# Tree attention on one core: loads of Q, K and V put in the order of their use, V copied by half batches

## The chip, the cores and the metric

One core of one Trainium2 chip. The metric is the device time of a launch in microseconds (us); times are medians of several runs, and ratios are taken between runs of the same rounds on the same chip. Engines are called as in the profile: PE is TensorE (PEld its weight loads), DVE is VectorE, ACT is ScalarE, POOL is GpSimd, SP issues the stores. The span is the time from the first to the last instruction of a profiled execution. A half-clock stretch is one in which the trace records a granted TensorE clock of 0.5.

## The reference

Attention over a sequence of 512 whose mask lets each position see itself and its ancestors in a binary tree. Q, K and V are float32, 8 batches x 12 heads x 512 x 64.

```python
mask = np.zeros((seq, seq))
for i in range(seq):
    mask[i, i] = 1
    parent = i
    while parent > 0:
        parent = (parent - 1) // 2
        mask[i, parent] = 1
scores = np.einsum('bhqd,bhkd->bhqk', Q, K) / np.sqrt(dim) + (1 - mask) * (-1e9)
weights = np.exp(scores - scores.max(-1, keepdims=True))
weights = weights / (weights.sum(-1, keepdims=True) + 1e-10)
return np.einsum('bhqk,bhkd->bhqd', weights, V).astype(np.float32)
```

## The kernel before

Work goes by pairs of heads, 6 pairs a batch, 48 in all. POOL issues the loads, which cast float32 to bf16 on the way (the page has 38.24 MB read from HBM and 18.88 MB in the queue of the loads). A load waits for the landing of the load eight places before it, so up to eight are on their way at any time: in the trace the 19th issue began at 27.73 us, 0.28 us after the landing of the 11th load at 27.45. For each pair PE transposes Q and K (`qt`, `kt` are copied out by DVE and ACT), computes scores, ACT exponentiates, PE multiplies with V, and DVE normalizes (`rec`, then `of` in two instructions). Because the mask needs only some keys, V is not used as loaded: DVE copies it into `v1` and `vx`, with 10 small instructions for any number of heads (two on 64 partitions, eight on 32).

```python
def load(b):
    qs = stage.tile([P, H, T * D], bf16); ks = ...
    if b == 0:
        plan = [(Q, b, 0, 2), (K, b, 0, 2), (V, b, 0, 6), (Q, b, 2, 6),
                (K, b, 2, 6), (V, b, 6, H), (Q, b, 6, H), (K, b, 6, H)]
    elif b == 1:
        plan = [(Q, b, 0, 6), (K, b, 0, 6), (V, b, 0, H), (Q, b, 6, H),
                (K, b, 6, H), (V, b + 1, 0, H)]
    elif b < B - 1:
        plan = [(Q, b, 0, 6), (K, b, 0, 6), (V, b + 1, 0, H),
                (Q, b, 6, H), (K, b, 6, H)]
    ...
# the order of work (ACT and PE inside these calls)
for i in range(N):
    b, hp = pairs[i]
    if i + 1 < N: scores(i + 1)
    if i + 3 < N: transposes(i + 3)       # needs Q and K of pair i + 3
    values(i)                             # PE, then rec, of, of on DVE, then the store
    if b == 0: ...
    elif b + 1 < B:                       # the copies of the next batch's V
        if hp == 0: todo = spread(b + 1, 0, H)
        cuts = (0, 1, 2, 4, 6, 8, 10)
        copies(todo[cuts[hp]:cuts[hp + 1]])
```

Of the kernel before, what the change touches and what calls it, by code (L numbers as in the profile page):

```python
# [126 lines left out]
def kernel(  # L127
# [8 lines left out]
    B, H, S, D = Q.shape  # L136
# [64 lines left out]
    def load(b):  # L201
        qs = stage.tile([P, H, T * D], bf16)
        ks = stage.tile([P, H, T * D], bf16)
        if b == 0:
            plan = [(Q, b, 0, 2), (K, b, 0, 2), (V, b, 0, 6), (Q, b, 2, 6),
                    (K, b, 2, 6), (V, b, 6, H), (Q, b, 6, H), (K, b, 6, H)]
        elif b == 1:
            plan = [(Q, b, 0, 6), (K, b, 0, 6), (V, b, 0, H), (Q, b, 6, H),
                    (K, b, 6, H), (V, b + 1, 0, H)]
        elif b < B - 1:  # L210
            plan = [(Q, b, 0, 6), (K, b, 0, 6), (V, b + 1, 0, H),
                    (Q, b, 6, H), (K, b, 6, H)]
        else:
            plan = [(Q, b, 0, 6), (K, b, 0, 6), (Q, b, 6, 10), (K, b, 6, 10),
                    (Q, b, 10, H), (K, b, 10, H)]
        for src, n, h0, h1 in plan:
            if src is V:
                if n not in loaded_v:
                    loaded_v[n] = stage.tile([P, H, T * D], bf16, name="vs")
                dst = loaded_v[n]  # L220
            else:
                dst = qs if src is Q else ks
            nc.gpsimd.dma_start(  # L223
                out=dst[:, h0:h1, :],
                in_=src[n, h0:h1].rearrange("h (p t) d -> p h (t d)", t=T),
            )
        loaded[b] = (qs, ks)

    def pick(v, t0, t1):

        stop = t1 + (1 if t1 > t0 else -1)
        return v[:, :, t0:stop if stop >= 0 else None:t1 - t0, :]

    def spread(b, h0, h1):
        vs = loaded_v[b]
        v1, vx = v1s[b % NV], vxs[b % NV]
        v = vs[:, h0:h1, :].rearrange("p h (t d) -> p h t d", t=T)
        ops = [
            (vx[64:P, h0:h1, 0:3:2, 0:D], v[64:P, :, 0:3:2, :]),
            (vx[0:64, h0:h1, 1:4:2, 0:D], v[64:P, :, 1:4:2, :]),  # L240
        ]
        for part, c, t0, t1 in ((0, 0, 1, 2), (32, 0, 3, 0), (64, 1, 2, 1),
                                (96, 1, 0, 3)):
            assert KORD[XW[c] + part // 32] == (t0, 1)
            assert KORD[XW[c + 2] + part // 32] == (t1, 1)
            ops.append((
                vx[part:part + 32, h0:h1, c:c + 3:2, 0:D],
                pick(v[32:64], t0, t1),
            ))
        for r in range(T):  # L250
            ops.append((
                v1[32 * r:32 * r + 32, h0:h1, 0:D],
                v[0:32, :, KORD[K1 + r][0], :],
            ))
        return ops

    def copies(ops):
        for o, i in ops:
            nc.vector.tensor_copy(out=o, in_=i)  # L259

    pairs = [(b, hp) for b in range(B) for hp in range(HP)]
    state = {}

    def transposes(i):
        b, hp = pairs[i]
        if hp == 0:
            load(b)
        qs, ks = loaded[b]
        tq = psumT.tile([P, 512], bf16)
        tk = psumT.tile([P, 576], bf16)  # L270

        def put(o, src, t, mat):
            for hi in range(2):
                nc.tensor.matmul(  # L274
                    out=o[D * hi:D * hi + D], rhs=perms[mat],
                    lhsT=src[:, 2 * hp + hi, D * t:D * t + D],
                    start=True, stop=True, is_transpose=True,
                )

        put(tq[:, 64:192], qs, 0, 1)  # L280
        put(tq[:, 0:384].rearrange("d (c x) -> d c x", c=2)[:, :, 0:64], qs, 1, 0)
        for t in range(2, T):
            put(tq[:, P * t:P * t + P], qs, t, 0)
        for t in range(T):
            at = kput[t][1]
            if at[1] - at[0] == 32:
                step, run = at[2] - at[0], 64
            else:
                step, run = at[1] - at[0], 32
                assert at[2] - at[1] == step  # L290
            o = tk[:, at[0]:]
            o = bass.AP(o.tensor, o.offset, [list(o.ap[0]), [step, P // run], [1, run]])
            put(o, ks, t, 2 + t)
        qt = work.tile([P, 512], bf16)
        kt = work.tile([P, 512], bf16)
        nc.vector.tensor_copy(out=qt[:, :], in_=tq[:, :])  # L296
        nc.scalar.copy(  # L297
            out=kt[:, :].rearrange("d (i j x) -> d i j x", j=2, x=32),
            in_=tk[:, :].rearrange("d (j i x) -> d i j x", j=2, x=32)[:, 0:8],
        )  # L300
        state[i] = (qt, kt)

    def scores(i):
        b, hp = pairs[i]
        q_, k_ = state[i]
        st1 = psumS.tile([P, 2, 512], fp32)
        stx = psumS.tile([P, 2, 512], fp32)

        def mm(dst, lhsT, rhs, first):
            nc.tensor.matmul(  # L310
                out=dst, lhsT=lhsT, rhs=rhs, start=first, stop=True,
                skip_group_check=not first,
            )

        hb = [slice(D * hi, D * hi + D) for hi in range(2)]
        q = [q_[hb[hi], :] for hi in range(2)]
        k = [k_[hb[hi], :] for hi in range(2)]
        for hi in range(2):
            mm(st1[:, hi, :], ck1[hb[hi], :], cq1[hb[hi], :], True)
        for hi in range(2):  # L320
            mm(st1[:, hi, :], k[hi][:, 32 * K1:32 * K1 + P], q[hi], False)
        et1 = et1pool.tile([P, 2, 512], bf16)
        nc.scalar.activation(  # L323
            out=et1[:, :, :], in_=st1[:, :, :], func=AF.Exp, scale=scale
        )
        for hi in range(2):
            mm(stx[:, hi, 0:384], ckx[hb[hi], :], cqx[hb[hi], :], True)
        for c in range(T):
            for hi in range(2):
                mm(stx[:, hi, 96 * c:96 * c + 96],  # L330
                   k[hi][:, 32 * XW[c]:32 * XW[c] + P],
                   q[hi][:, P * c + 32:P * c + P], False)
        etx = etxs[i % NX]
        nc.scalar.activation(  # L334
            out=etx[:, :, :, 32:P],
            in_=stx[:, :, 0:384].rearrange("p h (c q) -> p h c q", c=T),
            func=AF.Exp, scale=scale,
        )
        state[i] = (et1, etx)
# [35 lines left out]
    N = len(pairs)  # L375
    E = mybir.EngineType
    with tc.manual_schedule(engines={E.PE, E.DVE, E.Activation, E.Pool}):
        transposes(0)
        scores(0)
        transposes(1)  # L380
        copies(spread(0, 0, 6))
        transposes(2)
        for i in range(N):
            b, hp = pairs[i]
            if i + 1 < N:
                scores(i + 1)
            if i + 3 < N:
                transposes(i + 3)
            values(i)
            if b == 0:  # L390
                if hp in (0, 3):
                    todo = spread(0, 6, H) if hp == 0 else spread(1, 0, H)
                copies(todo[4 * (hp % 3):4 * (hp % 3) + 4])
            elif b + 1 < B:
                if hp == 0:
                    todo = spread(b + 1, 0, H)
                cuts = (0, 1, 2, 4, 6, 8, 10)
                copies(todo[cuts[hp]:cuts[hp + 1]])


# [28 lines left out]
```

## Time and profile before

| | before |
|---|---|
| time, median of 4 runs | 160.02 us (158.96 to 160.46) |
| profiled span | 159.3 us |
| DVE busy | 121.9 us |
| V copies on DVE | 90 |
| last load landed | 137.0 us |

Most lines that matter are shown in the prediction. One is kept for here: the chain that ended last, by engine. It is followed back from the last instruction, at each step to whatever released it.

```profile
DMA 63%; DVE 19%; PE 8%; POOL 4%; issue 3%; POOLq 0%
```

The chain goes back over some 50 us of work without waits for loads, to the K that landed at 109.64, and from there only from landing to landing. Read alone it says that loads set the time. DVE's timeline says that the engine was rarely short of work even so. Both are true of a kernel in which two resources are nearly in balance.

### The profile page before, as it was taken

What the parts mean: (1) busy time and instruction counts of PE and PEld (TensorE: products, weight loads), DVE (VectorE), ACT (ScalarE), POOL (GpSimd) and SP (SyncE); (2) the same over time, 40 slices, a digit from 0 to 9 for tenths busy, and PEclk for the clock granted to TensorE, in tenths of its full rate; (3) what the DMA queues carried; (4) which work ended last, traced back from release to release, by engine and by line L of the source; (5) the groups of instructions that cost most, each with busy time, mean ns of one, the idle gap of its engine ahead of it and who ended that gap; (6) DMA issues with size and microseconds to landing.
All of it is one profiled execution on the core that took longest, in us unless ns stands there. A gap on an engine that the chain in (4) does not pass through costs nothing.

```text
span 159.3 us, 5182 instructions
## 1 busy us (share of the span) xinstructions
PE 112.5 (71%) x2208; PEld 80.9 (51%) x2208; DVE 121.9 (77%) x291; ACT 107.5 (67%) x145; POOL 39.1 (25%) x49
## 2 busy tenths in 40 slices
PE   0357497743998789865996699644998599759730
PEld 0224365532766566543774467423676476547520
DVE  2109499899689989995799799971699989997651
ACT  3053559565488779882898689851598879887820
POOL 7965450422232233032212332203301000000000
PEclk9999969999599999998799999995599999999995
DMA  5999999999999999999999999999999999323331
GB/s 136 148 182 196 197 199 220 223 238 217 225 224 223 237 226 237 234 237 225 217 227 238 225 240 226 242 221 240 199 220 236 228 238 221 126 83 121 136 128 69
DMA packets 50951, 32.28 MB, mean 203 GB/s; under 512 B 1520, under 2 KB 50800, under 8 KB 50928
## 3 DMA queue, kind: packets, MB, share of 16 engines
q0 software_dynamic: 37584, 18.88, 87.6%
q1 hardware_dynamic: 13344, 13.08, 28.5%
q8 instruction: 17, 0.28, 0.7%
q14 instruction: 6, 0.05, 0.1%
HBM read 38.24 MB, written 12.58 MB: 319 GB/s over the span
## 4 chain that ended last, share of the span: by engine, by line
DMA 63%; DVE 19%; PE 8%; POOL 4%; issue 3%; POOLq 0%
DMA ks<-in_K_dram 44%; DMA qs<-in_Q_dram 19%; DVE of L363 11%; PE o L352 4%; DVE vx L259 3%; POOL qs L223 2%; DVE rec L358 2%; DVE v L259 2%; DVE qt L296 2%; POOL ks L223 1%; PE st L310 1%; POOL vs L223 1%; PE tk L274 1%; PE stx L310 1%; PE tq L274 1%
## 5 line engine op out<-in xcount | busy, mean ns | idle before, releaser
L323 ACT ACTIVATE et<-st 128x1024 bf16<-128x1024 f32 x48 | 49.2, 1025 | 26.5 <-PE st L310 26.0
L363 DVE TENSOR_TENSOR of<-o,rec 128x512 f32<-128x512 f32 x96 | 53.2, 554 | 3.3
L352 PE MATMUL o<-v,et 128*128 128x65 bf16 x384 | 31.8, 199 | 18.6 <-DVE of L363 12.2
L297 ACT COPY kt<-tk 128x512 bf16<-128x512 bf16 x48 | 28.4, 592 | 17.8 <-PE tk L274 17.8
L352 PEld LDWEIGHTS <-et 128*128 128x128 bf16 x384 | 25.9, 100 | 25.9 <-DVE of L363 16.8
L334 ACT ACTIVATE etx<-stx 128x768 bf16<-128x768 f32 x48 | 38.6, 805 | 0.0
L352 PE MATMUL o<-vx,etx 128*128 128x65 bf16 x384 | 31.5, 198 | 0.0
L274 PE MATMUL tq<-ptile,qs 128*64 128x128 bf16 x384 | 21.4, 237 | 13.5 <-DMA qs<-in_Q_dram 9.3
L296 DVE COPY qt<-tq 128x512 bf16<-128x512 bf16 x48 | 20.3, 422 | 13.1 <-PE tq L274 12.1
L259 DVE COPY vx<-vs 32x1536 bf16<-32x1536 bf16 (+3 forms) x54 | 28.5, 527 | 1.2
L274 PE MATMUL tk<-ptile,ks 128*64 128x128 bf16 x384 | 21.2, 235 | 9.8 <-DMA ks<-in_K_dram 9.5
L352 PEld LDWEIGHTS <-etx 128*128 128x128 bf16 x384 | 26.7, 100 | 0.0
L310 PEld LDWEIGHTS <-kt 64*128 64x128 bf16 x480 | 19.4, 100 | 9.5 <-issue 2.6
L223 POOL DMA_DIRECT2D qs<-in_Q_dram x18 | 15.1, 836 | 35.0 <-DMA vs<-in_V_dram 12.9
L274 PEld LDWEIGHTS <-qs 128*64 128x64 bf16 x384 | 14.9, 116 | 17.1 <-DMA qs<-in_Q_dram 10.5
L223 POOL DMA_DIRECT2D ks<-in_K_dram x18 | 15.1, 841 | 31.9 <-DMA ks<-in_K_dram 10.4
L358 DVE RECIPROCAL rec<-o 128x8 f32<-128x8 f32 x48 | 9.6, 200 | 15.0 <-PE o L352 15.0
L274 PEld LDWEIGHTS <-ks 128*64 128x64 bf16 x384 | 15.3, 119 | 11.2 <-DMA ks<-in_K_dram 10.8
L310 PE MATMUL st<-ctile 64*128 64x512 bf16 x96 | 20.2, 417 | 0.0
L310 PE MATMUL st<-qt,kt 64*128 64x512 bf16 x96 | 19.7, 407 | 0.1
L310 PE MATMUL stx<-qt,kt 64*128 64x96 bf16 x384 | 17.2, 212 | 0.0
L310 PE MATMUL stx<-ctile 64*128 64x384 bf16 x96 | 16.9, 348 | 0.0
(11 smaller groups left out, 35.7 us busy)
## 6 DMA issues: line engine op xcount, KB each, us to landing
out_dram<-of SPq DMA_DIRECT2D x48, 256.0 KB, 6.3
qs<-in_Q_dram POOLq DMA_DIRECT2D x14, 384.0 KB, 27.2
ks<-in_K_dram POOLq DMA_DIRECT2D x14, 384.0 KB, 26.2
vs<-in_V_dram POOLq DMA_DIRECT2D x7, 768.0 KB, 28.2
vs<-in_V_dram POOLq DMA_DIRECT2D x2, 384.0 KB, 8.4
qs<-in_Q_dram POOLq DMA_DIRECT2D x2, 256.0 KB, 15.4
ks<-in_K_dram POOLq DMA_DIRECT2D x2, 256.0 KB, 15.2
ctile<-tree_codes SPq DMA_DIRECT2D x1, 288.0 KB, 2.9
```

Source lines behind the costliest of these rows:

```text
L223: nc.gpsimd.dma_start(out=dst[:, h0:h1, :], in_=src[n, h0:h1].rearrange("h (p t) d -> p h (t d)", t=T),)
L259: nc.vector.tensor_copy(out=o, in_=i)
L274: nc.tensor.matmul(out=o[D * hi:D * hi + D], rhs=perms[mat], lhsT=src[:, 2 * hp + hi, D * t:D * t + D], start=True, stop=True, is_transpos ...
L296: nc.vector.tensor_copy(out=qt[:, :], in_=tq[:, :])
L297: nc.scalar.copy(out=kt[:, :].rearrange("d (i j x) -> d i j x", j=2, x=32), in_=tk[:, :].rearrange("d (j i x) -> d i j x", j=2, x=32)[:, 0:8],
L310: nc.tensor.matmul(out=dst, lhsT=lhsT, rhs=rhs, start=first, stop=True, skip_group_check=not first,)
L323: nc.scalar.activation(out=et1[:, :, :], in_=st1[:, :, :], func=AF.Exp, scale=scale)
L334: nc.scalar.activation(out=etx[:, :, :, 32:P], in_=stx[:, :, 0:384].rearrange("p h (c q) -> p h c q", c=T), func=AF.Exp, scale=scale,)
L352: nc.tensor.matmul(out=o2[:, hi, (D + 1) * t:(D + 1) * (t + 1)], lhsT=e, rhs=v, start=n == 0, stop=n == len(w) - 1,)
L358: nc.vector.reciprocal(out=rec[:, :, :, :], in_=o4[:, :, :, D:D + 1])
L363: nc.vector.tensor_tensor(out=of4[p0:p1, :, t0, :], in0=o4[p0:p1, :, c0, 0:D], in1=rec[p0:p1, :, c0, :].to_broadcast([p1 - p0, 2, t0.stop, ...
```

## The change

The intent is that no load stands in the queue ahead of one needed sooner: for each group of three pairs Q, K, then V. Since V now comes only a group ahead of its use, it can no longer be copied for a whole batch at a time. It is copied by half batches, over the three pairs ahead of its use; the copies of one half batch, with the pairs that they are laid over, are called a spread below.

```diff
--- before.py
+++ after.py
@@ -203,16 +203,14 @@
         ks = stage.tile([P, H, T * D], bf16)
         if b == 0:
             plan = [(Q, b, 0, 2), (K, b, 0, 2), (V, b, 0, 6), (Q, b, 2, 6),
-                    (K, b, 2, 6), (V, b, 6, H), (Q, b, 6, H), (K, b, 6, H)]
-        elif b == 1:
-            plan = [(Q, b, 0, 6), (K, b, 0, 6), (V, b, 0, H), (Q, b, 6, H),
-                    (K, b, 6, H), (V, b + 1, 0, H)]
-        elif b < B - 1:
-            plan = [(Q, b, 0, 6), (K, b, 0, 6), (V, b + 1, 0, H),
-                    (Q, b, 6, H), (K, b, 6, H)]
+                    (K, b, 2, 6)]
         else:
-            plan = [(Q, b, 0, 6), (K, b, 0, 6), (Q, b, 6, 10), (K, b, 6, 10),
-                    (Q, b, 10, H), (K, b, 10, H)]
+            plan = [(Q, b, 0, 6), (K, b, 0, 6), (V, b, 0, 6)]
+        if b < B - 1:
+            plan += [(Q, b, 6, H), (K, b, 6, H), (V, b, 6, H)]
+        else:
+            plan += [(V, b, 6, H), (Q, b, 6, 10), (K, b, 6, 10),
+                     (Q, b, 10, H), (K, b, 10, H)]
         for src, n, h0, h1 in plan:
             if src is V:
                 if n not in loaded_v:
@@ -387,15 +385,12 @@
             if i + 3 < N:
                 transposes(i + 3)
             values(i)
-            if b == 0:
-                if hp in (0, 3):
-                    todo = spread(0, 6, H) if hp == 0 else spread(1, 0, H)
-                copies(todo[4 * (hp % 3):4 * (hp % 3) + 4])
-            elif b + 1 < B:
-                if hp == 0:
-                    todo = spread(b + 1, 0, H)
-                cuts = (0, 1, 2, 4, 6, 8, 10)
-                copies(todo[cuts[hp]:cuts[hp + 1]])
+            if i - i % 3 + 3 < N:
+                if i % 3 == 0:
+                    nb, nh = pairs[i + 3]
+                    todo = spread(nb, 2 * nh, 2 * nh + 6)
+                cuts = (0, 3, 6, 10)
+                copies(todo[cuts[i % 3]:cuts[i % 3 + 1]])
 
 
 # ---- launch: one core; inputs and outputs as the reference has them ----
```

> **What bounds the kernel now.** I read the page first (engines, slices), then the waits, then VectorE's timeline, then the groups by form and the trace's landing of every load.
>
> ```profile
> PE 112.5 (71%) x2208; PEld 80.9 (51%) x2208; DVE 121.9 (77%) x291; ACT 107.5 (67%) x145; POOL 39.1 (25%) x49
> PEclk9999969999599999998799999995599999999995
> DMA  5999999999999999999999999999999999323331
> ```
>
> The queues are full until slice 34 (136 us), where the last loads land, yet the kernel runs 23 us longer. So transfers do not set the end directly. DVE is the busiest engine at 77%. The clock row shows short stretches at half speed.
>
> ```profile
> ACT et L323 <- PE st L310: 26.0, 29, 3.2
> DVE rec L358 <- PE o L352: 15.0, 17, 3.4
> PE tk L274 <- DMA ks<-in_K_dram: 9.5, 7, 2.3
> ```
>
> DVE's waits in the middle of the run are few. The longest one, 3.4 us, is this, in DVE's timeline (start, duration):
>
> ```profile
> 105.75 0.72 DVE L259 COPY v<-vs 32x768 bf16<-32x768 bf16 x2
> 107.50 0.42 DVE L296 COPY qt<-tq 128x512 bf16<-128x512 bf16 x1 [1.03 <-PE tq L274]
> 111.35 0.21 DVE L358 RECIPROCAL rec<-o 128x8 f32<-128x8 f32 x1 [3.43 <-PE o L352]
> ```
>
> TensorE waited there for Q and K of batch 5's second half, queued behind the whole V of batch 6; that K landed at 109.64. This is what the change aims at. Away from such places DVE runs without a gap:
>
> ```profile
> 46.29 0.19 DVE L358 RECIPROCAL rec<-o 128x8 f32<-128x8 f32 x1
> 46.51 1.14 DVE L363 TENSOR_TENSOR of<-o,rec 128x512 f32<-128x512 f32 x2
> 47.69 1.11 DVE L259 COPY vx<-vs 32x1536 bf16<-32x1536 bf16 x2
> 48.83 0.42 DVE L296 COPY qt<-tq 128x512 bf16<-128x512 bf16 x1
> 49.17 0.20 DVE L358 RECIPROCAL rec<-o 128x8 f32<-128x8 f32 x1
> ```
>
> One pair takes 1.76 us of fixed DVE work plus its share of V copies, here 2.88 in all. The last pairs, which have no copies, come every 2.14 us, TensorE's own pace. So the kernel is bound by DVE almost throughout, with a few transfer stalls on top. I model it as a chain of output issues, read from the trace: first at 21.1 us; batch 0's six periods 19.4 (they carry one and a half batches of V copies); batches 1 to 6 at 15.6 each (measured undisturbed in batch 6: 2.33, 2.21, 2.89, 2.90, 2.37, 2.88); five periods of 2.14; 3.35 from the last output to the end. Sum 148.0. Losses, as excess of single periods: waits for K 1.6 + 0.4 + 3.4 = 5.4; half-clock stretches 4.3; V copies held up beside load issues about 2. That makes 159.7 against 159.3 measured, so the chain holds.
>
> [...] both queues' packet time is 87.6% and 28.5% of the span, over 100% together; [...]
>
> ```profile
> L259 DVE COPY vx<-vs 32x1536 bf16<-32x1536 bf16 x28 | 15.5, 554 | 0.6
> L259 DVE COPY v<-vs 32x768 bf16<-32x768 bf16 x28 | 10.3, 369 | 0.4
> L259 DVE COPY v<-vs 32x384 bf16<-32x384 bf16 x8 | 2.8, 349 | 0.1
> ```
>
> Half of 554 is 277, but a free 768 copy takes 0.353 us and a free 384 copy 0.25 (the 349 holds collisions). [...] beside the load issue at 27.73 two small copies took 0.83 us,
>
> ```profile
> 27.78 0.83 DVE L259 COPY v<-vs 32x384 bf16<-32x384 bf16 x2
> 25.49 0.51 DVE L259 COPY v<-vs 32x384 bf16<-32x384 bf16 x2
> ```
>
> against 0.51 for two with no issue beside them. [...] a copy that writes partitions 0 up right before the qt copy lets qt start 0.08 early (45.95, while the copy runs to 46.03); where the copy ends in a higher quadrant qt starts 0.03 late.
>
> **The change part by part.**
>
> *Loads.* The bytes stay 37.7 MB read. Groups of three pairs get Q, K, V in order, 384 KB each. From 22.6 to 130.8 us before, 38 such units landed, 2.85 us each, so a group lands every 8.54. Batch 0's second Q and K move ahead of its V by one unit: K lands at 16.66, not 18.62. TensorE does these transposes before the first values, but the tq buffer is free only at 16.97, so the first output comes at 19.7: **1.4 us gained**. Placing the new order on the measured landings by bytes, group 3's K lands at 30.2 and is needed at 34.8; group 6's at 56.3, needed at 61.5; group 12's at 109.6, needed at 114.9. Each V lands 3 us later and is needed 2.7 us later. So there are four to five us in hand everywhere and the **5.4 us of waits for K go**.
>
> *Copies.* Batches 1 to 7 have 10 copies each, all heads at once; batch 0 has 20. Now every batch has 20: 160 instead of 90. A full batch costs 6 x 0.554 + 4 x 0.353 = 4.74 us; two halves cost 2 x (6 x 0.353 + 4 x 0.25) = 6.24, with 0.013 between copies some 6.4. Seven batches: **about +11.4 us of DVE work**, on the engine that sets the pace.
>
> *Wait at the end of each spread.* TensorE's values of the next group read v1, which the last copies finish. Before, at each batch end, the period was 2.88 with only 0.73 of copies: copies, then 0.67 of matmuls, then the reciprocal. That is 2.15 + copies rather than 1.76 + copies. It now comes 15 times rather than 8: about +2.7.
>
> *Periods.* Pair 0 of a group: 1.76 + 3 x 0.366 - 0.10 (qt not held) = 2.76. Pair 1: 2.86. Pair 2: 2.15 + 4 x 0.264 - 0.11 (first v copy not held) = 3.10. A group takes **8.72 us**, 2.91 per pair, against 15.6/6 = 2.60.
>
> *Sum.* 19.7 + 15 groups x 8.72 (130.8) + 2 x 2.14 + 3.35 = 158.1 us undisturbed. Half-clock stretches: a throttled pair took 3.4 to 3.6 before, so each costs 0.6 instead of 1.1 to 1.3; I take 2.0. Copies beside load issues: [...] Over a period of 2.95 the chance times the cost is 0.11 us an issue; some 36 issues follow 19 us, a few in idle time, so 3.4 (my estimate). Span 163.5; the timed median was 0.5 above the profiled span, so **164.0 us**.
>
> **Rivals.**
> *The stalls go and little is paid.* If DVE had slack for the extra copies, 159.8 - 5.4 - 1.4 = 153. For it: DVE is at 77%, and in the chain of waits DMA has 63%. Against: that chain strings landings together, each behind the load eight places before, and the periods show DVE without a gap outside some ten places.
> *V just in time becomes a new wait.* DVE now waits in line for each V at pair 0 of the group ahead. At 8.72 us of work for 8.54 us of transfer it is close to balance; if loads slow to 3.1 us a unit, the last V lands near 145, and with three pairs with and three without copies behind it the time is about 162: not far from mine by another mechanism. Against: the lead of 4 us from the start, which grows.
> *Few collisions.* From 42 to 120 us before, issues cost copies only 0.25 us in 26 issues (one copy or two in a row, luck of phase). Then 160.5 to 161.5: within 2%.
> *Phases lock.* Issues and pairs both recur every 2.9 us; if they lock badly, 0.3 x 36 gives 11 us and 170.
>
> **Range and chances.** The base 158.1 is good to 1.5, the clock to 1, the collisions to 2.5, together about 3: 160.5 to 167.5. Two per cent faster (under 156.6) would need less than the undisturbed chain, chance 0.04. Slower starts at 163.0, just under my value: 0.60; the same 0.36.
>
> **What would show it.** DVE copies of V x160, no 1536 form, busy of DVE near 133 us; the first output near 19.7; DVE's rec waits short, with none of 3.4 us behind a landing; outputs every 8.7 to 9 us a group from 20 to 150; loads landing well before use and the DMA row falling off near 136 again, with compute 25 us behind. Wrong if DVE sits idle for V or K (rival two), if groups take under 8.5 us, or if small copies beside load issues last no longer than free ones.

## The result

| | before | after |
|---|---|---|
| time, median of 4 runs | 160.02 us (158.96 to 160.46) | 164.8 us (164.11 to 165.57) |
| profiled span | 159.3 us | 162.3 us |
| DVE busy | 121.9 us | 131.3 us |
| V copies on DVE | 90 | 160 |
| last load landed | 137.0 us | 137.0 us |
| first output issued | 21.1 us | 20.1 us |

The ratio is 1.031, 95% interval 1.023 to 1.039: 3% slower. (A ratio is the mean time of one kernel's fast runs over that of the other's of the same rounds, so it is not quite the ratio of the medians quoted.)

The engines, the clock and the DMA row of the changed kernel's page:

```profile
PE 112.3 (69%) x2208; PEld 81.4 (50%) x2208; DVE 131.3 (81%) x361; ACT 106.5 (66%) x145; POOL 42.4 (26%) x56
PEclk9999999699999999999999598799999999999695
DMA  5999999999999999999999999999999996123131
```

The queues run dry at the same time as before, at 137 us; the work ends 25 us later instead of 22. The chain that ended last has turned over:

```profile
DVE 65%; PE 19%; issue 7%; DMA 5%; POOL 1%; DVEq 0%; POOLq 0%
```

From the first output on there is no landing left in it. The waits (total, times, longest) show what took the place of the wait for K:

```profile
PE o L350 <- DVE v L257: 25.4, 15, 2.3
...
DVE rec L356 <- PE o L350: 9.2, 21, 1.2
...
PE tk L272 <- DMA ks<-in_K_dram: 1.0, 2, 0.7
```

PE's wait for K is down from 9.5 us to 1.0, and `rec` no longer waits over 1.2 us anywhere. PE now waits 15 times for the v copies, once for each group. DVE's timeline of one group, from the first copies of one to those of the next (start, duration):

```profile
38.61 1.09 DVE L257 COPY vx<-vs 64x768 bf16<-64x768 bf16 x3
39.63 0.40 DVE L294 COPY qt<-tq 128x512 bf16<-128x512 bf16 x1
...
41.35 1.08 DVE L257 COPY vx<-vs 32x768 bf16<-32x768 bf16 x3
42.47 0.42 DVE L294 COPY qt<-tq 128x512 bf16<-128x512 bf16 x1
...
44.11 1.03 DVE L257 COPY v<-vs 32x384 bf16<-32x384 bf16 x4
45.17 0.42 DVE L294 COPY qt<-tq 128x512 bf16<-128x512 bf16 x1
45.89 0.21 DVE L356 RECIPROCAL rec<-o 128x8 f32<-128x8 f32 x1 [0.30 <-PE o L350]
...
47.31 1.09 DVE L257 COPY vx<-vs 64x768 bf16<-64x768 bf16 x3
```

DVE works without a gap but one: after the four v copies and `qt` it waits 0.30 us for the values of the next group, which could not begin before those copies ended. (PE's 25 us of waits for the copies are no measure of the loss: in e3 below they are gone, and PE waits 30.7 us for `of` instead.) In the first period `qt` starts 0.07 us before the three copies in front of it end, in the second 0.04 after; the last copy writes from partition 0 in the one case and from a higher one in the other, the same two cases as in the prediction. In this trace `qt` started 0.07 us early each of the 15 times that it followed such a copy to partition 0; what causes this was not shown. The group takes 8.70 us, and so does each of the next three.

The same copies by form (busy, mean ns of one, idle before):

```profile
L257 DVE COPY vx<-vs 32x768 bf16<-32x768 bf16 x64 | 23.5, 367 | 1.1
L257 DVE COPY v<-vs 32x384 bf16<-32x384 bf16 x64 | 16.9, 265 | 0.7
L257 DVE COPY vx<-vs 64x768 bf16<-64x768 bf16 x32 | 11.4, 357 | 0.7
```

They add up to 51.8 us, where the copies before (all six forms) added up to 41.5. A free copy of 768 elements takes 0.351 us and one of 1536 elements 0.551, so an estimate of the fixed part of a copy is 2 x 0.351 - 0.551 = 0.15 us; 70 more copies at 0.15 are 10.5 us, about the 10.3 of the difference.

### The profile page after: what moved, and what is told of

The parts are those of the page before. It is cut to its first block, busy times and chain, and to the rows that moved or that the text cites. A ratio compares the mean times of both kernels' runs of the same rounds, so it can differ in the third digit from the quotient of the medians.

```text
span 162.3 us, 5259 instructions
## 1 busy us (share of the span) xinstructions
PE 112.3 (69%) x2208; PEld 81.4 (50%) x2208; DVE 131.3 (81%) x361; ACT 106.5 (66%) x145; POOL 42.4 (26%) x56
## 4 chain that ended last, share of the span: by engine, by line
DVE 65%; PE 19%; issue 7%; DMA 5%; POOL 1%; DVEq 0%; POOLq 0%
DVE of L361 29%; DVE vx L257 15%; PE o L350 11%; DVE v L257 10%; DVE qt L294 6%; DMA qs<-in_Q_dram 5%; DVE rec L356 4%; PE st L308 3%; PE tq L272 2%; PE stx L308 2%; PE tk L272 1%; POOL qs L221 1%; POOL vs L221 1%; POOL ks L221 0%; DVEq L361 0%
## 5 line engine op out<-in xcount | busy, mean ns | idle before, releaser
L257 DVE COPY vx<-vs 32x768 bf16<-32x768 bf16 (+1 forms) x96 | 34.9, 364 | 1.8
L294 DVE COPY qt<-tq 128x512 bf16<-128x512 bf16 x48 | 20.1, 418 | 11.3 <-PE tq L272 10.4
L272 PE MATMUL tk<-ptile,ks 128*64 128x128 bf16 x384 | 21.1, 235 | 1.3 <-DMA ks<-in_K_dram 1.0
L221 POOL DMA_DIRECT2D qs<-in_Q_dram x18 | 14.6, 814 | 26.3 <-DMA ks<-in_K_dram 18.8
L221 POOL DMA_DIRECT2D vs<-in_V_dram x16 | 13.4, 835 | 27.2 <-DMA qs<-in_Q_dram 19.1
L257 DVE COPY v<-vs 32x384 bf16<-32x384 bf16 x64 | 16.9, 265 | 0.7
```

The costliest lines, as they stand in the source:

```text
L221: nc.gpsimd.dma_start(out=dst[:, h0:h1, :], in_=src[n, h0:h1].rearrange("h (p t) d -> p h (t d)", t=T),)
L257: nc.vector.tensor_copy(out=o, in_=i)
L272: nc.tensor.matmul(out=o[D * hi:D * hi + D], rhs=perms[mat], lhsT=src[:, 2 * hp + hi, D * t:D * t + D], start=True, stop=True, is_transpos ...
L294: nc.vector.tensor_copy(out=qt[:, :], in_=tq[:, :])
```

## The experiments

Theory: the change loses through its copies (70 more instructions, each with a fixed cost, on the engine that sets the pace, and a spread that ends right before its use), while its order of loads by itself gains. Main rival: V just in time is the loss, through new waits for loads. Seven kernels and one repetition ran. The times of the kernel before in these rounds were 159.1 to 163.8 us, its fast runs 159.1 to 161.6. The kernels were timed in rounds other than those of the changed kernel, so where two ratios are set against each other, the rounds differ.

### e1: one step of the new order alone

Edit of the kernel before:

```diff
         elif b < B - 1:
-            plan = [(Q, b, 0, 6), (K, b, 0, 6), (V, b + 1, 0, H),
-                    (Q, b, 6, H), (K, b, 6, H)]
+            plan = [(Q, b, 0, 6), (K, b, 0, 6), (Q, b, 6, H),
+                    (K, b, 6, H), (V, b + 1, 0, H)]
```

> The kernel before with one thing of the new order: in batches 2 to 6 the second half of Q and K is issued ahead of the next batch's V. Copies stay as before (whole batches, 90 copies, 10 a batch). Theory (the change lost through its copies, not through its order): DVE work stays at 122 us, the 3.4 us wait for K of batch 5 goes, but the whole V now lands last of its batch, and the first copy of it may wait about 2.7 us at the first pair of each batch. Counted from landings (a batch of loads every 17.1 us) the end comes at a span of 150 to 156, timed 152 to 158, so 1 to 5% faster than before. Rival (order of use by itself makes new waits for V and costs as much as it saves): 160 to 165, with DVE waiting for V in most batches.

Measured: 158.84 us, ratio to before 0.994 (0.988 to 1.000), span 156.9. The order does not cost, but a gain is hardly clear of the noise (the verdict by the 2% line is the same time), and it is less than expected: time and span lie just outside the expected ranges. The wait of 3.4 us is gone (no `rec` waits over 2.2 us), and a part of it has come back as a wait for V. DVE's timeline where batch 6 begins:

```profile
123.76 1.14 DVE L363 TENSOR_TENSOR of<-o,rec 128x512 f32<-128x512 f32 x2
126.44 0.56 DVE L259 COPY vx<-vs 64x1536 bf16<-64x1536 bf16 x1 [1.54 <-DMA vs<-in_V_dram]
```

The first copy of the last V waited 1.54 us for that V, which landed at 126.4, and 30 us of work follow it. So the rival has something in it, for an order that loads V whole.

### e2: the new copies alone

The loads of the kernel before, with the changed kernel's loop:

```diff
-            if b == 0: ...
-            elif b + 1 < B: ...
+            if i - i % 3 + 3 < N:
+                if i % 3 == 0:
+                    nb, nh = pairs[i + 3]
+                    todo = spread(nb, 2 * nh, 2 * nh + 6)
+                cuts = (0, 3, 6, 10)
+                copies(todo[cuts[i % 3]:cuts[i % 3 + 1]])
```

> The loads of the kernel before, the copies of the changed kernel (160 half-batch copies spread over the three pairs ahead of use). Theory (the copies carry the loss): the groups take 8.7 us as in the changed kernel, first output near 21, so timed 164 to 167.5, the same as the changed kernel or up to 1.5% slower. At 17.4 us of DVE work a batch against 17.1 us of loads most of the 5.4 us of waits for K disappear even with the old order. Rival (the loss comes from the order of the loads, V just in time): near the kernel before, 159 to 161.

Measured: 167.71 us, ratio 1.049 (1.041 to 1.058). So the copies alone cost 4.9%, about 7.9 us of 160.2. The change as a whole costs 3.1%; by these two ratios the order of the loads gives back 1.8%, about 2.9 us, beside these copies. (The two ratios come from different rounds; their intervals do not overlap.) The time is just above the expected range. I had expected most of the waits for K to be absorbed, and they were not. The waits of e2:

```profile
PE o L352 <- DVE v L259: 22.0, 13, 2.3
...
DVE rec L358 <- PE o L352: 12.1, 20, 2.2
...
PE tk L274 <- DMA ks<-in_K_dram: 6.7, 5, 2.3
```

PE still waited 6.7 us for K, against 1.0 in the changed kernel and 9.5 before.

### e3: the same copies one pair earlier

Edit of the changed kernel (`load` of a batch is called a little sooner in the program so that its V exists; the order of the issues is the same):

```diff
-            if i - i % 3 + 3 < N:
-                if i % 3 == 0:
-                    nb, nh = pairs[i + 3]
+            j = i + 1
+            if j - j % 3 + 3 < N:
+                if i == 0 or j % 3 == 0:
+                    nb, nh = pairs[j - j % 3 + 3]
                     todo = spread(nb, 2 * nh, 2 * nh + 6)
                 cuts = (0, 3, 6, 10)
-                copies(todo[cuts[i % 3]:cuts[i % 3 + 1]])
+                copies(todo[0 if i == 0 else cuts[j % 3]:cuts[j % 3 + 1]])
```

> The changed kernel with each group's copies moved one pair earlier, so that the four v copies end a pair before TensorE's values read them. Same 160 copies, same loads in the same order. Theory (each spread that ends right before its use costs 2.15 - 1.76 = 0.39 us, 15 times): group 8.3 us instead of 8.7, timed 157.5 to 160.5, some 3% faster than the changed kernel; TensorE's waits for the v copies (25 us in all) fall to near nothing. Rival (transfers set the pace, V just in time): needing V 3 us earlier makes DVE wait for it, and the time stays at 164 or rises.

Measured: 159.22 us, ratio 0.998 (0.990 to 1.007), span 157.4: 3.3 points under the changed kernel's ratio, with the same 160 copies and the same loads. DVE's timeline of a group there:

```profile
76.73 1.03 DVE L257 COPY v<-vs 32x384 bf16<-32x384 bf16 x4
77.79 0.42 DVE L294 COPY qt<-tq 128x512 bf16<-128x512 bf16 x1
78.14 0.20 DVE L356 RECIPROCAL rec<-o 128x8 f32<-128x8 f32 x1
```

`rec` follows `qt` with no wait, and outputs come every 8.31 us a group (68.52, 76.83, 85.14, 93.45). Fifteen times 0.39 is 5.9 us; from the first to the 46th output the traces have 127.7 us here and 133.9 in the changed kernel, while the first output came 1.1 us later here. So the wait at the end of each spread is real and of the size predicted, though it costs DVE nothing that its busy time would show. The two executions also differ in their clock (0.98 here, with no half-clock stretch between 21 and 151 us, and 0.944 there), but the 8.31 and the 8.70 are both read where nothing disturbs the groups.

The rival's waits for V do not appear: DVE has none on a V in this trace. From 28 to 43 us five pairs took 15.05 us where undisturbed ones take 13.90, with DVE at work without a gap; the 1.15 us more are five V copies that lasted longer beside load issues. One of them is among these three (at 73.98 three such copies took 1.08 us):

```profile
31.24 1.32 DVE L257 COPY vx<-vs 32x768 bf16<-32x768 bf16 x3
```

In the whole trace 14 copies after 19 us were prolonged, by 2.5 us together.

### e4: without the v copies (wrong result on purpose)

```diff
-        nc.vector.memset(v1s[i][:, :, D:VW], 1.0)
+        nc.vector.memset(v1s[i][:, :, :], 1.0)
...
-                copies(todo[cuts[i % 3]:cuts[i % 3 + 1]])
+                copies(todo[cuts[i % 3]:min(6, cuts[i % 3 + 1])])
```

> Wrong result on purpose: the changed kernel without the 4 v copies of each group (after batch 0's first half), the v tiles filled with ones once. Loads unchanged. Theory (DVE sets the pace of the changed kernel, and right under it lie the loads): DVE work of a group falls to 1.76 + 1.1 + 1.76 + 1.1 - 0.1 plus 2.14 = 7.8 us, less than the 8.54 us of a group's loads, so now loads bind: waits for Q and K at group starts, DMA busy to about 137, end about 12 us behind the last landing: timed 150 to 154. Rival (loads or V just in time bind the changed kernel already): 162 to 165.

Measured: 157.81 us, ratio 0.985 (0.979 to 0.992), span 155.9. The result was wrong, as intended. The ratio is 4.6 points under that of the changed kernel, so DVE did set the pace of the changed kernel. (Against the kernel before, the 2% line leaves the verdict unclear.) But 60 copies of 0.25 us and fifteen waits of 0.39 are 21 us, and only some 7 came back. The waits show where the rest stayed:

```profile
PE tk L272 <- DMA ks<-in_K_dram: 7.1, 9, 1.4
...
DVE vx L257 <- DMA vs<-in_V_dram: 2.5, 6, 0.8
```

With only a little less work on DVE the loads bind. My expected 150 to 154 was too low: the last load landed at 139.1, not 137, and the span ended 17 us behind it, not 12, because two pairs with copies and a half-clock stretch (137.8 to 141.2 us) still lay in the tail. A second thing shows here. In this trace 18 V copies after 19 us lasted longer than their form does otherwise, 4.6 us in all; in the changed kernel it was 5 copies and 1.4 us. One of them is among the copies of the first fence, with the load issue beside it in the second:

```profile
60.87 1.29 DVE L257 COPY vx<-vs 64x768 bf16<-64x768 bf16 x3 [0.56 <-DMA vs<-in_V_dram]
```

```profile
61.13 0.88 POOL L221 DMA_DIRECT2D ks<-in_K_dram  x1 [2.18 <-DMA vs<-in_V_dram]
```

The same landing of V released the copies and the next load issue, so they met. DVE waited for the landing of a V at six places in this trace. This is one way in which the two fall into step, and not the only one: e3 has 14 such copies without any wait for V, while e1 and e5 to e7, with 90 to 100 copies, most of them larger, have 3 to 7.

### e5, e6, e7: towards a version that beats both

e5 takes e1 and treats only the last batch's V as the change does: in halves, the second half behind the last batch's first Q and K.

```diff
-                    (K, b, 6, H), (V, b + 1, 0, H)]
+                    (K, b, 6, H), (V, b + 1, 0, H if b + 2 < B else 6)]
...
-            plan = [(Q, b, 0, 6), (K, b, 0, 6), (Q, b, 6, 10), (K, b, 6, 10),
-                    (Q, b, 10, H), (K, b, 10, H)]
+            plan = [(Q, b, 0, 6), (K, b, 0, 6), (V, b, 6, H), (Q, b, 6, 10),
+                    (K, b, 6, 10), (Q, b, 10, H), (K, b, 10, H)]
...
+            elif b + 2 >= B:
+                if hp == 0:
+                    todo = spread(B - 1, 0, 6) if b + 1 < B else spread(b, 6, H)
+                cuts = (0, 0, 3, 6, 8, 10, 10) if b + 1 < B else (0, 5, 10, 10, 10, 10, 10)
+                copies(todo[cuts[hp]:cuts[hp + 1]])
```

> e1 (Q and K of the second half ahead of the next batch's whole V, whole-batch copies for batches 1 to 6), with the last batch's V alone loaded and copied in halves as in the changed kernel: first half in batch 6, second half behind the last batch's first Q and K, copied over its first two pairs. Theory (in e1 the end hangs on the landing of the whole last V at 126.4 us, with 15.6 us of DVE work for a batch and 14 us of tail behind it; half of it lands 3 us earlier and half the copies move to where DVE has slack): span 153.5 to 156, timed 155.3 to 158, 2 to 3% faster than the kernel before. Rival (order and granularity of V at the end do not matter, e1 is bound by something else): within 0.5% of e1, so 0.99 to 1.0 of before.

Measured: 159.16 us, ratio 0.987 (0.982 to 0.993), span 156.2. It is 1.3% faster than the kernel before, which is clear of the noise but under the 2% line; the timed value is above the expected range, and at 158.5 to 159.4 its runs lie beside those of e1 (158.4 to 159.8); a gain over e1 is not shown.

e6 also moves batch 0's second Q and K ahead of its second V:

```diff
-                    (K, b, 2, 6), (V, b, 6, H), (Q, b, 6, H), (K, b, 6, H)]
+                    (K, b, 2, 6), (Q, b, 6, H), (K, b, 6, H), (V, b, 6, H)]
```

> e5 with batch 0's second Q and K ahead of its second V, as in the changed kernel. Theory: the first output comes 1.4 us earlier, but in the middle of the run loads bind (a batch per 17.1 us against 15.6 of DVE work), so the end moves by less than 1 us against e5: 0 to 0.6% faster than e5. Rival (DVE binds throughout, so a gain at the start is kept to the end): 1.4 us, 0.9% faster than e5.

Measured: 159.70 us (18 runs), ratio 0.995 (0.991 to 0.999). The first output came at 18.8 us instead of e5's 21.3, but at the first output of batch 2 e6 was at 56.95 to e5's 56.83, and at that of batch 6 at 125.3 to 125.2. The gain at the start was used up on the way, and the end was no earlier: the ratio is 0.8 points above e5's, where 0 to 0.6% faster had been expected, though the intervals just overlap. That loads took the gain, as expected, is not shown. From 32 to 44 us, where most of it went, e6 has no wait of PE or DVE for a load; it has a half-clock stretch of 10.2 us (32.4 to 42.6; e5 has 3.4 us there), in which `rec` waited 1.7 us for PE, and one copy prolonged by 0.2 us beside a load issue.

e7 lets the copies of batches 2 to 6 begin two pairs later, so as not to wait for V:

```diff
-                cuts = (0, 1, 2, 4, 6, 8, 10)
+                cuts = (0, 0, 0, 3, 6, 8, 10)
```

> e6 with the copies of batches 2 to 6 begun at the third pair of the batch instead of the first. Theory (in e5 and e6 the whole V, landing last of its batch's loads, is waited for by the first copy: the V of batch 6 at 108.9 us, and 16.2 us of DVE work behind it set the output at 125.2, although Q and K had landed five us before): the output at the start of batch 6 comes at 123 to 124, the end two us earlier, span near 154.5, timed 156 to 158, 2 to 3% faster than the kernel before. Rival (a later start of the copies only packs them into fewer pairs and costs as much as it saves): 159 to 161, the same as e6 or slower.

Measured: 160.15 us (22 runs), ratio 0.996 (0.993 to 0.999): the same as e6, and the rival was right. The output at the start of batch 6 came at 126.1, not 123 to 124. DVE no longer waited for a V (2.9 us in e6), but two pairs without copies leave it idle:

```profile
111.29 0.41 DVE L296 COPY qt<-tq 128x512 bf16<-128x512 bf16 x1
112.12 0.21 DVE L358 RECIPROCAL rec<-o 128x8 f32<-128x8 f32 x1 [0.42 <-PE o L352]
112.36 1.14 DVE L363 TENSOR_TENSOR of<-o,rec 128x512 f32<-128x512 f32 x2
113.53 1.69 DVE L259 COPY vx<-vs 64x1536 bf16<-64x1536 bf16 x3
```

A pair without copies takes PE's 2.14 us, so 0.4 us of DVE time is lost in it, and the four other pairs carry more. Batches 2 to 5 took 16.9 to 17.7 us each, about the 17.1 us of a batch's loads; which of the two set them is not separated. The ratios of e1, e5, e6 and e7 lie within 1% of each other.

### The changed kernel again

> The changed kernel once more, for a second trace. Theory: DVE group period 8.7 us where nothing disturbs it, whatever the clock and the phase do; the time copies lose beside load issues depends on how issue and copy phases drift, 1.4 us in the first trace between 20 and 150 us, and may be anything from 0.5 to 4 here. Rival (collisions are fixed by the program): 1.4 us again at the same pairs.

Measured once, without rounds: 161.99 us, span 160.2. Where nothing disturbs it the group takes 8.70 us again (37.13 to 45.83). Prolonged copies after 19 us cost 1.0 us, at other places than before (three between 22 and 28 us, two at 101 and 104), so collisions are not fixed by the program. This execution had its first output at 18.8 us and fewer half-clock stretches before the end than the first; a single run doesn't settle how often. Its time is below all four timed runs (164.1 to 165.6), beside a kernel before whose fast runs were 159.1 to 161.4 in the rounds of that chip. So the loss may be smaller in some executions than the 3.1%; one run of unknown state cannot say. Of the 2.1 us between the two spans 1.3 lie before the first output.

## Why the prediction was right

It forecast 164.0 us, slower, and 164.8 was measured. The mechanism is the one that it named; that the total came so near is in part luck, since two errors, of 1.3 and 2.0 us, went in opposite directions (the last points). By its steps:

- **First output** at 19.7: 20.1 in the profiled run, 18.8 in the second trace.
- **Periods** 2.76, 2.86 and 3.10 us, group 8.72: measured 2.74, 2.86 and 3.09, group 8.69 (output issues at 38.61, 41.35, 44.21, 47.30). This carried the prediction, and it rested on durations that batch 0 of the kernel before already showed for half-batch copies.
- **Waits for K vanish**: right. V was in hand too: the copies at 47.31 used a V landed at 42.28, those at 110.09 one landed at 101.70. The hand was 5 us and grew to 8.
- **DVE work**, +11.4 us with the gaps between copies: the copies' own time rose by 10.3 (10.5 by its sum without gaps), DVE's busy time to 131.3, not 133.
- **The wait at the end of each spread**, 0.39 us fifteen times: shown by e3.
- **The copies cost more than the order gains**: shown by e2. That the order gains beside these copies follows from e2 and the change itself. In the traces of e2 and of the changed kernel, whose spans differ by 2.4 us, 1.2 lie before the first output and 1.4 between it and the 46th; the latter hold half-clock stretches too, so the share of the waits for K is not separated.
- **Collisions of copies with load issues**, 3.4 us: mis-sized, 1.4 measured (1.0 in the second trace). The 0.11 us an issue behind it was my estimate, with issues and copies taken to meet at random. Between 42 and 71 us issues came every 2.87 us and pairs every 2.90, so that they drifted past each other slowly, and no copy was prolonged; of the five that were, three stood between 91 and 98 us. In e4, e3 and e2 it was 4.6, 2.5 and 1.4 us, so the guess was not off everywhere.
- **Half-clock stretches**, 2.0: the outputs from first to 46th took 133.9 us; fifteen groups of 8.70 are 130.5, collisions 1.4, which leaves 2.0. About 1.4 of it lies in or beside the stretches that the clock records show, and 0.5 at the first pair, where PE was late. From the 46th output to the end it took 8.3 us, not 7.6, with 4.9 of them at half clock.
- **From span to time** I added 0.5 us. In the four runs of the changed kernel the time is 1.8 above the span each time. The 0.5 compared the median with a profiled execution that was itself longer (161.44 us). This error of 1.3 us and that of the collisions, 2.0, cancelled for the most part.

The rival in which DVE has slack (153) was wrong. V just in time did not bind the changed kernel; it did in e1 and e4, where DVE's work is smaller. Few collisions was the case, but did not bring the four runs within 2%, as that rival had it; the single later run, 161.99, comes near its 160.5 to 161.5. The rival in which phases lock (170) did not come true.

## What to carry to other kernels

Putting loads in the order of use gained little here (0.6% alone, hardly clear of the noise, and by ratios of different rounds 1.8% beside the half-batch copies); count first what the finer grain adds on the engine that works without gaps, here 70 instructions with a fixed cost of about 0.15 us each (the estimate above, from copies of 0.351 and 0.551 us). When work is spread over the time ahead of its use, let it end one step early: a spread that ends right before its reader cost 0.39 us each time (8.70 us a group against 8.31 in e3), which no busy time shows. A chain of waits made of landings does not prove that loads bind, when the timeline of an engine beside it has no gaps.

## What the traces show of copies and load issues

- A copy with no issue beside it took 0.251 us for 384 elements a partition, 0.351 to 0.357 for 768 and 0.551 to 0.556 for 1536 (medians by form, in the kernel before and in the changed kernel). Twice 0.251 less 0.351 gives 0.15 us again for the fixed part, the same estimate as from 768 and 1536.
- In the kernel before, beside a load issue of 0.82 us at 27.735, a copy that began 0.05 us into it took its free 0.251 us, and one that began 0.31 us into it took 0.564, ending 0.06 us after the issue. In the traces of the kernel before and of the changed kernel, copies that began up to 0.08 us into an issue of 0.82 took their free time; those that began 0.24 to 0.57 us into it lasted longer, and ended 0.05 to 0.06 us (384 elements), 0.15 to 0.16 (768) or 0.35 to 0.36 (1536) after its end, which is each time their free time less 0.20. So an estimate from these is that such an issue kept copies from starting from at latest 0.24 to about 0.62 us into it, not for the whole 0.82 that the profile gives it.
- Load issues and copies can fall into step: 18 prolonged copies (4.6 us) in e4, where at one place the same landing is seen to release both, and 14 (2.5 us) in e3, against 5 (1.4 us) in the changed kernel.
